# Gate and up of both feed-forward layers as seven block products over two token halves, with the activations kept in DRAM and the down projection as a phase of its own

## The chip, the cores and the metric

The kernel runs on one core of one Trainium2 chip. The time is the device time of one execution in microseconds (us); the times given are the median of several runs. The profile is one further execution, recorded by the hardware profiler.

Engines in the profile: PE is TensorE, whose matmuls do most of the arithmetic, and PEld its weight load; DVE is VectorE, ACT ScalarE, POOL GpSimd, and SP SyncE, which issues the transfers. SBUF is the on-chip memory of the engines, PSUM the accumulators that TensorE writes.

## The reference

Two layers, each a token mixer followed by a SwiGLU feed-forward part, with a norm before and after each. Layer 0 mixes with a gated linear recurrence (RG-LRU), layer 1 with a state-space scan (SSD). There are 1024 prompt tokens and 8 x 16 sample tokens, T = 1152 in all, D = 1024 features and a feed-forward width of 2816 = 22 x 128.

```python
def swiglu(h, w_gate, w_up, w_down):
    return (jax.nn.silu(h @ w_gate) * (h @ w_up)) @ w_down

    ...
        x = x + rmsnorm(mix, p['norm_mix_post'][layer])
        hn = rmsnorm(x, p['norm_ffn_pre'][layer])
        f = swiglu(hn, p['ffn_w_gate'][layer], p['ffn_w_up'][layer], p['ffn_w_down'][layer])
        x = x + rmsnorm(f, p['norm_ffn_post'][layer])
```

Everything is float32, and the products are computed close to float32 accuracy.

## The kernel before

Activations lie with features on the 128 partitions and tokens along the columns. Every float32 operand of a product is split in two parts of TensorE's faster type fp32r: a rounded high part (names ending in h) and the rest (ending in l). A product then takes three matmuls, high by high, high by low and low by high (`mm3`). A weight unit is 128 x 1024: it is loaded raw (`wr`), ScalarE casts its high part (`wh`), and VectorE subtracts for the low part (`wl`). `plan` lists the units in their order of use, and `ahead` and `prepare` keep two raw ones and up to four split ones in flight.

Tokens are worked in three blocks of 384 (`TB`). `gemm` runs 8 feature blocks x 3 matmuls into one of four PSUM buffers named `mm`. In `ffn` (line 783), `up_tb` (line 790) computes for one of the 22 feature tiles and one block the gate and the up product (24 matmuls each), scales the gate by the norm factor `rstd`, applies silu, multiplies by the up product and the factor, and splits the result into `ah` and `al`, which stay in SBUF. `down_tb` (line 804) multiplies a pair of feature tiles by the down weights. The output rows `acc` gather eleven such pairs: the first is copied in by ScalarE, the others are added by VectorE. Down products stand between the up products of the next pairs; the last two pairs are merged, block by block, with `boundary` (line 542).

`boundary` ends a part of a layer for one token block: it normalises the new rows (`mix` or `acc`), adds them to the residual `x`, stores `x`, scales it by the next norm's gain and splits it into `hl`, feature block by feature block. The next layer part's products read `hl`. The factor of the next norm is worked out meanwhile (`npre`, `rs`) and applied to the products.

No instruction is issued where it stands in the program. A recorder takes every operation with the ranges that it reads and writes, computes a latest start for each from an estimate of its cost, counted back from TensorE's sequence, and hands this as a priority to a scheduler, which simulates the engines and fixes the order on each. All instructions thus have the profile's line L330. Each engine then works through its list in order and waits where an operand isn't ready. A tile's buffer comes from a pool with a set number of buffers, and a new tile waits until the last reader of the old one is done: 17 rows of 1180 float32 columns (`rp`), three pairs for `hl` (`ap`).

## Time and profile before

| | before |
| --- | --- |
| median of three runs | 3095.74 us (3092.99 to 3096.46) |
| the profiled execution | 3090.76 us, span 3088.6 us |
| mean granted TensorE clock | 0.981 |
| TensorE busy | 3002.2 us, 17659 matmuls |
| VectorE, ScalarE, GpSimd busy | 1776.4, 965.5, 76.8 us |
| moved by DMA | 263.21 MB, 85 GB/s over the span |
| first and second feed-forward layer | 859.60 and 858.10 us |

A row of the groups gives engine, operation, written tile, read tiles, shape, type and count, then the busy time in us and the mean of one in ns, then the engine's idle time ahead of these instructions and what ended it. A row of the timeline gives start and duration in us; a bracket holds the wait just before it. A row of the stretches gives each engine's busy time in us with its count, the granted clock, and the share and rate of the DMA engines.

### The profile page before, as it was taken

How to read it: one execution, taken by the hardware profiler on the slowest of the kernel's cores; microseconds unless marked ns; L12 is line 12 of the kernel's file. 1: busy time of each engine (PE TensorE's matmuls, PEld its weight loads, DVE VectorE, ACT ScalarE, POOL GpSimd, SP SyncE). 2: the span in 40 equal slices, each digit the busy share in tenths (PEclk: the TensorE clock that was granted, in tenths of full speed). 3: DMA queues.
4: the chain of work that ended last, by engine and by line, in shares of the span. 5: the costliest groups of instructions: out<-in, count | busy, mean ns of one | idle time of the engine just before them, and what ended most of it. 6: DMA issues, size and time to landing. Idle time of an engine off the chain costs nothing.

```text
span 3088.6 us, 42956 instructions
## 1 busy us (share of the span) xinstructions
PE 3002.2 (97%) x17659; PEld 2920.6 (95%) x17659; DVE 1776.4 (58%) x3432; ACT 965.5 (31%) x1441; POOL 76.8 (2%) x176
## 2 busy tenths in 40 slices
PE   8999999999999999999989999999999999999997
PEld 8999999999999999889877988899999999999997
DVE  7765472444444445869978887733663444444436
ACT  5783343111111113445433444322332111111121
POOL 0300000000000000000000000000000000000000
PEclk9999999999999999899999999999999999999998
DMA  3111231111111111335554655432211111111113
GB/s 130 43 35 42 95 111 41 41 42 42 42 41 46 44 44 70 135 116 172 168 169 133 199 174 182 181 134 81 91 67 41 42 41 48 43 42 41 42 35 123
DMA packets 176036, 263.21 MB, mean 85 GB/s; under 512 B 19136, under 2 KB 130112, under 8 KB 175840
## 3 DMA queue, kind: packets, MB, share of 16 engines
q1 hardware_dynamic: 175840, 260.47, 25.0%
q8 instruction: 139, 2.28, 0.3%
q14 instruction: 57, 0.47, 0.0%
HBM read 198.46 MB, written 61.97 MB: 84 GB/s over the span
## 4 chain that ended last, share of the span: by engine, by line
PE 88%; DVE 7%; DMA 2%; ACT 1%; issue 1%; SPq 0%; DVEq 0%; ACTq 0%
PE mm L330 82%; PE aux L330 5%; DVE core L330 1%; DVE acc L330 1%; DVE x L330 1%; DVE hl L330 1%; DMA core<-acd 1%; DVE xc L330 1%; PE one L330 1%; DMA ysc<-core 1%; DMA core<-xbc 1%; DVE wl L330 1%; DVE npre L330 1%; DVE sb L330 0%; DVE silu L330 0%
## 5 line engine op out<-in xcount | busy, mean ns | idle before, releaser
L330 PE MATMUL mm<-hl,wh 128*128 128x384 f32 x7728 | 1991.5, 338 | 30.4 <-DVE hl L330 13.2
L330 PEld LDWEIGHTS mm<-hl,wh 128*128 128x128 f32 x7728 | 1406.2, 190 | 43.2 <-DVE hl L330 18.5
L330 PE MATMUL mm<-hl,wl 128*128 128x384 f32 x3864 | 1294.9, 337 | 0.0
L330 PEld LDWEIGHTS mm<-hl,wl 128*128 128x128 f32 x3864 | 731.5, 189 | 2.7 <-issue 2.7
L330 ACT CAST wh<-wr 128x1024 fp32r<-128x1024 f32 (+1 forms) x218 | 228.2, 1047 | 739.6 <-PE mm L330 737.6
L330 DVE TENSOR_TENSOR acc<-acc,mm 128x384 f32<-128x384 f32 x456 | 248.8, 552 | 199.2 <-PE mm L330 197.5
L330 DVE TENSOR_TENSOR wl<-wr,wh 128x1024 fp32r<-128x1024 f32 (+1 forms) x218 | 265.3, 1217 | 167.4 <-ACT wh L330 167.2
L330 PE MATMUL mm<-ah,wh 128*128 128x384 f32 x1056 | 352.8, 339 | 0.0
L330 PE MATMUL mm<-al,wh 128*128 128x384 f32 x1056 | 350.8, 337 | 0.0
L330 PE MATMUL mm<-ah,wl 128*128 128x384 f32 x1056 | 350.2, 336 | 0.0
L330 DVE TENSOR_TENSOR silu<-silu,mm 128x384 f32<-128x384 f32 x132 | 73.0, 553 | 381.6 <-PE mm L330 380.4
L330 PEld LDWEIGHTS mm<-al,wh 128*128 128x128 f32 x1056 | 198.0, 188 | 0.0
L330 PEld LDWEIGHTS mm<-ah,wh 128*128 128x128 f32 x1056 | 197.9, 188 | 0.0
L330 PEld LDWEIGHTS mm<-ah,wl 128*128 128x128 f32 x1056 | 197.7, 188 | 0.0
L330 DVE TENSOR_TENSOR silu<-mm,rstd 128x384 f32<-128x384 f32 x132 | 73.5, 557 | 211.1 <-PE mm L330 211.1
L330 ACT CAST ah<-silu 128x384 fp32r<-128x384 f32 x132 | 67.8, 514 | 357.3 <-DVE silu L330 357.3
L330 ACT ACTIVATE silu<-silu 128x384 f32<-128x384 f32 x132 | 69.1, 523 | 265.2 <-DVE silu L330 265.2
L330 DVE SCALAR_TENSOR_TENSOR xc<-pad,pvt,xc 128x1176 f32<-128x1176 f32 x96 | 137.1, 1434 | 18.5 <-ACT xc L330 17.9
L330 PE MATMUL aux<-core,core 128*64 128x128 f32 (+1 forms) x1088 | 106.2, 310 | 10.4 <-DVE core L330 6.6
L330 ACT ACT_TABLE_LOAD x74 | 94.9, 1283 | 67.0 <-DVE xc L330 28.9
L330 DVE TENSOR_TENSOR al<-silu,ah 128x384 fp32r<-128x384 f32 x132 | 73.3, 555 | 46.4 <-ACT ah L330 46.4
L330 PEld LDWEIGHTS aux<-core,core 128*64 128x64 f32 (+1 forms) x1088 | 67.5, 145 | 29.2 <-issue 17.2
(142 smaller groups left out, 2351.4 us busy)
## 6 DMA issues: line engine op xcount, KB each, us to landing
wr<-in_wu SPq DMA_DIRECT2D x216, 512.0 KB, 3.5
core<-acd SPq DMA_DIRECT2D x36, 512.0 KB, 5.0
xbc<-pad SPq DMA_DIRECT2D x24, 576.0 KB, 3.3
core<-xbc SPq DMA_DIRECT2D x36, 384.0 KB, 3.7
xs<-x SPq DMA_DIRECT2D x18, 576.0 KB, 3.0
x<-xs SPq DMA_DIRECT2D x18, 576.0 KB, 6.4
ysc<-core SPq DMA_DIRECT2D x36, 256.0 KB, 4.0
y<-ysc SPq DMA_DIRECT2D x16, 576.0 KB, 5.9
```

The source lines that it names most:

```text
L330: op.ins = getattr(getattr(self.nc, op.engine), op.name)(*op.args, **op.kw).ins
```

## The change

Tokens are cut in four quarters of 288 (`QB`), two to each half of 576 (`TH`). The boundaries ahead of the two feed-forward layers still work on blocks of 384, but write their split result into quarters (`Across`, `Quarters`), in two pieces per feature block.

Feature tiles 0 to 3 are computed as before, on quarters, in the order: tiles 0 and 1 on quarters 0 and 1, tiles 2 and 3 on all four, tiles 0 and 1 on quarters 2 and 3, for which their weights are loaded again. For tiles 4 to 21, gate and up together form the product of a 2 x 2 arrangement of weight blocks (gate or up, by half of the features) with a 2 x 2 arrangement of activation blocks (half of the features, by half of the tokens). `strassen` computes it in the form of Strassen and Winograd with seven block products of 12 matmuls instead of eight, once for each quarter of a half (j = 0, 1). It needs sums of activation blocks (`sums`: `x` is loaded back from DRAM, scaled by the gain, added and split; eight times per layer) and sums of weight blocks (`pump`: on GpSimd, in place in the raw tiles, then split into seven items). It combines the products with additions on VectorE and GpSimd (`ep`). Weights are now handled in halves of 512 columns everywhere.

The activations go to DRAM (`act`), in stores of 288 columns, not into `ah` and `al`. After the last tile the down projection runs as a second phase in six chunks, one of two feature tiles and five of four: `load` brings the activations back, ScalarE casts them, VectorE subtracts. The first chunk is copied into `acc` by ScalarE, and the last is merged with `boundary`.

The pools change with it (32 rows; eight half units of `wh` and `wl`, four raw); some parameters of the SSD part are loaded later into the place of others, and the sample states' decay (`bds`) moves into spare columns of other rows.

```diff
+QB = 288
+TH = T // 2
...
-NGF = NFF // 2
+NF0 = 4
+CHUNKS = [[0]] + [[2 * c + 1, 2 * c + 2] for c in range(5)]
...
+        r = [(n, l, f) for f in (0, 1, 2, 3, 0, 1, *range(4, NFF)) for n in ("fg", "fu")]
+        return r + [("fd", l, b, h) for bs in CHUNKS for h in range(2) for b in bs]
...
+        self.cuts = []
+        a, end = tb * TB, (tb + 1) * TB
+        while a < end:
+            b = a // QB
+            e = min(end, (b + 1) * QB)
+            self.cuts.append((Quarters(tiles, b), slice(a - tb * TB, e - tb * TB), slice(a - b * QB, e - b * QB)))
+            for half in range(2):
+                for lo in range(2):
+                    if (b, half, lo) not in tiles:
+                        tiles[b, half, lo] = t.row(F32R, "hq")
+            a = e
...
-        self.wp = ctx.enter_context(tc.tile_pool(name="wp", bufs=4))
-        self.ap = ctx.enter_context(tc.tile_pool(name="ap", bufs=3))
-        self.rp = ctx.enter_context(tc.tile_pool(name="rp", bufs=17))
+        self.wp = ctx.enter_context(tc.tile_pool(name="wp", bufs=8))
+        self.rp = ctx.enter_context(tc.tile_pool(name="rp", bufs=32))
...
+    def half(self, tag, dt):
+        return self.get(self.wp, tag, 512, dt, tag, 4 if tag == "wr" else 8)
...
+    def split_w(self, r):
+        nc = self.nc
+        h, l = self.half("wh", F32R), self.half("wl", F32R)
+        nc.scalar.copy(h, r)
+        nc.vector.tensor_tensor(out=l, in0=r, in1=h.bitcast(F32), op=SUB)
+        return h, l
+    def pump(self):
+        if self.n_entry == len(self.entries):
+            return
+        self.fill()
+        G = self.nc.gpsimd
+        e = self.n_entry
+        u, n = self.entries[e]
+        r, j = self.raws[e], self.n_item
+        done = self.preps.setdefault(u, [])
+        if n == 1:
+            done.append(self.split_w(r[j]))
+        else:
+            b11, b21, b12, b22 = r
+            src = (b11, b12, b12, b21, b11, b21, b22)[j]
+            sub = lambda out, x, y: G.tensor_tensor(out=out, in0=x, in1=y, op=SUB)
+            if j == 1:
+                sub(b11, b12, b11)
+                sub(b12, b22, b12)
+            elif j == 2:
+                sub(b12, b22, b11)
+            elif j == 5:
+                sub(b21, b21, b12)
+            done.append(self.split_w(src))
+        self.n_item += 1
+        if self.n_item == (2 if n == 1 else 7):
+            self.n_item = 0
+            self.n_entry += 1
+            self.raws.pop(e)
+            self.raw_out -= 2 * n
+            self.fill()
...
+    def sums(self, l, j, k, xin, gpre):
+        nc = self.nc
+        V = nc.vector
+        t = self.row(s="sx")[:, :4 * QB]
+        v = t.rearrange("p (i h t) -> p i h t", i=2, h=2)
+        for i in range(2):
+            t0 = i * TH + j * QB
+            nc.sync.dma_start(v[:, i], xin[:, k::4, t0:t0 + QB])
+        for h in range(2):
+            nc.scalar.activation(v[:, :, h], v[:, :, h], AF.Copy, scale=self.pv("g", gpre * 8 + k + 4 * h))
+        a11, a12, a21, a22 = (t[:, n * QB:(n + 1) * QB] for n in range(4))
+        V.tensor_tensor(out=a22, in0=a21, in1=a22, op=ADD)
+        V.tensor_tensor(out=a21, in0=a11, in1=a21, op=SUB)
+        V.tensor_tensor(out=a11, in0=a22, in1=a11, op=SUB)
+        V.tensor_tensor(out=a12, in0=a12, in1=a11, op=SUB)
+        h, lo = self.row(F32R, "sh")[:, :4 * QB], self.row(F32R, "sl")[:, :4 * QB]
+        nc.scalar.copy(h, t)
+        nc.vector.tensor_tensor(out=lo, in0=t, in1=h.bitcast(F32), op=SUB)
+        return {n: tuple(a[:, i * QB:(i + 1) * QB] for a in (h, lo)) for i, n in enumerate(("s2", "s4", "s3", "s1"))}
+    def ffn(self, l, quarters, xin, xout, gin, gpre):
+        nc = self.nc
+        V, A, G = nc.vector, nc.scalar, nc.gpsimd
         self.rs = self.rs_next
...
+        blocks = [Quarters(quarters, b) for b in range(4)]
+        def store(f, t0, a):
+            nc.sync.dma_start(self.act[l][:, f, t0:t0 + QB], a)
+        def up_tb(wg, wu, f, b):
+            pg, pu = self.gemm(wg, blocks[b]), self.gemm(wu, blocks[b])
+            t = self.tmp(QB, s="silu")
+            self.times_rs(t, pg[:, :QB], b * QB, QB)
             A.activation(t, t, AF.Silu)
...
+            V.tensor_tensor(out=t, in0=t, in1=pu[:, :QB], op=MUL)
+            self.times_rs(t, t, b * QB, QB)
+            store(f, b * QB, t)
+        def strassen(w, f, j, step):
+            e = self.row(s="ep")
+            e0, e1, e2, e3 = (e[:, n * QB:(n + 1) * QB] for n in range(4))
+            t1, t2 = j * QB, TH + j * QB
+            X, W = self.psm()[:, :QB], self.psm()[:, :QB]
+            def prod(i, ps, of, first=True):
+                step()
+                wh, wl = w[i]
+                for k in range(4):
+                    c = slice(k * P, (k + 1) * P)
+                    rh, rl = of(k)
+                    mm = nc.tensor.matmul
+                    mm(ps, wh[:, c], rh, start=first and k == 0, stop=False, skip_group_check=True)
+                    mm(ps, wh[:, c], rl, start=False, stop=False, skip_group_check=True)
+                    mm(ps, wl[:, c], rh, start=False, stop=k == 3, skip_group_check=True)
+            plain = lambda b, h: lambda k: tuple(blocks[b].part(4 * h + k, q) for q in range(2))
+            sm = lambda n: lambda k: S[j, k][n]
+            prod(0, X, plain(j, 0))
+            A.copy(e0, X)
+            prod(1, W, sm("s3"))
+            A.copy(e1, W)
+            Y = self.psx()[:, :QB]
+            prod(2, Y, sm("s2"))
+            V.tensor_tensor(out=e0, in0=e0, in1=Y, op=ADD)
+            prod(3, X, plain(j, 1), False)
+            self.times_rs(e3, X, t1, QB)
+            A.activation(e3, e3, AF.Silu)
+            prod(4, W, sm("s1"), False)
+            V.tensor_tensor(out=e2, in0=e0, in1=W, op=ADD)
+            G.tensor_tensor(out=e0, in0=e0, in1=e1, op=ADD)
+            G.tensor_tensor(out=e1, in0=e2, in1=e1, op=SUB)
+            N = self.psx()[:, :QB]
+            prod(5, N, plain(2 + j, 1))
+            V.tensor_tensor(out=e0, in0=e0, in1=N, op=ADD)
+            self.times_rs(e0, e0, t2, QB)
+            A.activation(e0, e0, AF.Silu)
+            V.tensor_tensor(out=e0, in0=e0, in1=e2, op=MUL)
+            self.times_rs(e0, e0, t2, QB)
+            store(f, t2, e0)
+            Q = self.psm()[:, :QB]
+            prod(6, Q, sm("s4"))
+            V.tensor_tensor(out=e1, in0=e1, in1=Q, op=ADD)
+            V.tensor_tensor(out=e1, in0=e1, in1=e3, op=MUL)
+            self.times_rs(e1, e1, t1, QB)
+            store(f, t1, e1)
+        for tb in range(NTB):
+            self.norms[id(blocks[tb])] = self.pres[tb]
+        S = {}
+        for fs, bs in (((0, 1), (0, 1)), ((2, 3), range(4)), ((0, 1), (2, 3))):
+            ws = [(self.take("fg", l, f), self.take("fu", l, f, ahead=f != fs[-1])) for f in fs]
+            for b in bs:
+                for w, f in zip(ws, fs):
+                    up_tb(*w, f, b)
+                    if b == 3 and f == 0:
+                        for _ in range(4):
+                            self.pump()
+            if 2 in fs:
+                for k in range(4):
+                    S[0, k] = self.sums(l, 0, k, xin, gin)
+        for k in range(4):
+            S[1, k] = self.sums(l, 1, k, xin, gin)
+        for f in range(NF0, NFF):
+            w = self.take("fg", l, f)
+            for j in range(2):
+                strassen(w, f, j, self.pump if j else lambda: None)
+        res = []
+        def load(bs):
+            r = []
+            for f in (2 * b + q for b in bs for q in range(2)):
+                a, h, lo = self.row(s="act"), self.row(F32R, "ah"), self.row(F32R, "al")
+                nc.sync.dma_start(a[:, :T], self.act[l][:, f, :])
+                A.copy(h[:, :T], a[:, :T])
+                V.tensor_tensor(out=lo[:, :T], in0=a[:, :T], in1=h[:, :T].bitcast(F32), op=SUB)
+                r.append((h, lo))
+            return r
+        def down_tb(ws, act, h, tb, first):
             c = slice(tb * TB, (tb + 1) * TB)
             for m in range(4):
                 ps = self.psm()
...
+                n = len(act)
+                for q in range(n):
+                    wh, wl = ws[q // 2][q % 2]
+                    cs = slice(m * P, (m + 1) * P)
+                    self.mm3(ps[:, :TB], wh[:, cs], wl[:, cs], act[q][0][:, c], act[q][1][:, c], q == 0, q == n - 1)
                 d = 4 * h + m
...
+                if first:
                     A.copy(acc[d][:, c], ps[:, :TB])
                 else:
                     V.tensor_tensor(out=acc[d][:, c], in0=acc[d][:, c], in1=ps[:, :TB], op=ADD)
...
+        act = load(CHUNKS[0])
+        acc = [self.row(s="acc") for _ in range(KD)]
+        for n, bs in enumerate(CHUNKS):
+            if n < len(CHUNKS) - 1:
+                nxt = load(CHUNKS[n + 1])
+                for h in range(2):
+                    wd = [self.take("fd", l, b, h) for b in bs]
+                    for tb in range(NTB):
+                        down_tb(wd, act, h, tb, n == 0)
+                act = nxt
                 continue
...
+            wd = [[self.take("fd", l, b, h) for b in bs] for h in range(2)]
             for tb in range(NTB):
...
                 for h in range(2):
...
+                    down_tb(wd[h], act, h, tb, False)
+                res.append(self.boundary(tb, acc, xin, l * 4 + 3, gpre, xout))
         return res
```

The order changes most clearly at three places. The first is VectorE's list at the entry of the first feed-forward layer, where the second token block's boundary (`mix`, `x`) splits its result. Before, with `hl` as the split, and `silu` and `al` of the first feature tiles between:

```order
L330 TENSOR_TENSOR x_514<-x_514,mix_451 128x384
L330 SCALAR_TENSOR_TENSOR hl_528<-x_514,pvt,hl_528 128x384
L330 SCALAR_TENSOR_TENSOR mix_452<-mix_452,pvt,aux_516 128x384
L330 TENSOR_TENSOR al_552<-silu_563,ah_551 128x384
L330 TENSOR_TENSOR npre_529<-npre_529,npre_533 128x384
L330 TENSOR_TENSOR silu_566<-silu_566,mm_565 128x384
L330 TENSOR_TENSOR x_515<-x_515,mix_452 128x384
L330 SCALAR_TENSOR_TENSOR hl_528<-x_514,pvt,hl_528 128x384
L330 SCALAR_TENSOR_TENSOR mix_453<-mix_453,pvt,aux_516 128x384
```

And now, with quarters `hq`:

```order
L330 TENSOR_TENSOR x_612<-x_612,mix_571 128x384
L330 SCALAR_TENSOR_TENSOR hq_630<-x_612,pvt,hq_629 128x192
L330 SCALAR_TENSOR_TENSOR mix_572<-mix_572,pvt,aux_614 128x384
L330 SCALAR_TENSOR_TENSOR hq_598<-x_612,pvt,hq_597 128x192
L330 SCALAR_TENSOR_TENSOR rs_655<-rs_655 128x3
L330 TENSOR_TENSOR wl_703<-wr_682,wh_702 128x512
L330 TENSOR_TENSOR npre_631<-npre_631,npre_635 128x384
L330 TENSOR_TENSOR x_613<-x_613,mix_572 128x384
L330 SCALAR_TENSOR_TENSOR hq_630<-x_612,pvt,hq_629 128x192
L330 SCALAR_TENSOR_TENSOR mix_573<-mix_573,pvt,aux_614 128x384
```

Each feature block's split is now two rows of 192 columns for two quarters, and a weight split `wl` stands between the pieces.

The second is VectorE in the middle of a feed-forward layer: before, an up product's steps behind the acc adds,

```order
L330 TENSOR_TENSOR acc_619<-acc_619,mm_883 128x384
L330 TENSOR_TENSOR wl_903<-wr_887,wh_902 128x1024
L330 TENSOR_TENSOR silu_894<-mm_892,rstd_497 128x384
L330 TENSOR_TENSOR silu_894<-silu_894,mm_893 128x384
L330 TENSOR_TENSOR silu_894<-silu_894,rstd_497 128x384
L330 TENSOR_TENSOR al_891<-silu_894,ah_890 128x384
L330 TENSOR_TENSOR silu_897<-mm_895,rstd_497 128x384
```

and now the second quarter of one block-product tile, whose sums (`ep`, from PSUM tiles `mm` and `aux`) alternate with the weight splits of the next tile:

```order
L330 TENSOR_TENSOR wl_990<-wr_976,wh_989 128x512
L330 TENSOR_TENSOR ep_984<-ep_984,aux_991 128x288
L330 TENSOR_TENSOR wl_993<-wr_976,wh_992 128x512
L330 TENSOR_TENSOR wl_995<-wr_975,wh_994 128x512
L330 TENSOR_TENSOR ep_984<-mm_985,rstd_624 128x288
L330 TENSOR_TENSOR wl_997<-wr_974,wh_996 128x512
L330 TENSOR_TENSOR ep_984<-ep_984,mm_986 128x288
L330 TENSOR_TENSOR wl_1000<-wr_975,wh_999 128x512
L330 TENSOR_TENSOR ep_984<-ep_984,aux_998 128x288
```

The acc adds are gone from here, and a weight split comes with nearly every product.

The third is ScalarE at the first down products, which `COPY acc` takes out of PSUM. Before:

```order
L330 CAST wh_629<-wr_609 128x1024
L330 COPY acc_594<-mm_593 128x384
L330 CAST ah_579<-silu_589 128x384
L330 COPY acc_596<-mm_595 128x384
L330 COPY acc_598<-mm_597 128x384
L330 COPY acc_600<-mm_599 128x384
```

And now:

```order
L330 ACTIVATE ep_1344<-ep_1344 128x288
L330 CAST ah_1385<-act_1384 128x1152
L330 CAST ah_1388<-act_1387 128x1152
L330 CAST ah_1391<-act_1390 128x1152
L330 CAST ah_1394<-act_1393 128x1152
L330 COPY acc_1376<-mm_1396 128x384
L330 COPY acc_1377<-mm_1397 128x384
L330 COPY acc_1378<-mm_1398 128x384
```

Four casts of reloaded activations now stand directly ahead of the first copy. On GpSimd, 288 additions and subtractions are new, in a list that had 180 rows.

More of the change, by code (lines that the diff above doesn't have):

```diff
@@ L113 @@
 NPV = _o
+LRU0, SSD0, DT0 = PV["lcw"][0], PV["scw"][0], PV["dtb"][0]
+NPK = LRU0 + max(SSD0 - LRU0, DT0 - SSD0)
 CS = {}
@@ L339, in inside, with __init__, part, pieces @@
     return all(y0 <= x0 and x1 <= y1 for (x0, x1), (y0, y1) in zip(c, b))
+class Block:
+    n = TB
+    def __init__(self, t, s="hl"):
+        self.t = [t.row(F32R, s) for _ in range(5)] + [t.get(t.tp, "last", TB, F32R, s, 3)]
+    def part(self, k, lo):
+        i = k + 8 * lo
+        return self.t[i // 3][:, i % 3 * TB:(i % 3 + 1) * TB]
+    def pieces(self, k):
+        return [(slice(0, TB), self.part(k, 0), self.part(k, 1))]
+class Quarters:
+    n = QB
+    def __init__(self, tiles, b):
+        self.tiles, self.b = tiles, b
+    def part(self, k, lo):
+        return self.tiles[self.b, k // 4, lo][:, k % 4 * QB:(k % 4 + 1) * QB]
+class Across:
+    def __init__(self, t, tiles, tb):
+        self.cuts = []
[9 more added lines that the diff above has]
+            a = e
+    def pieces(self, k):
+        return [(src, q.part(k, 0)[:, dst], q.part(k, 1)[:, dst]) for q, src, dst in self.cuts]
 class Trunk:
@@ new lines, in fill @@
+    def fill(self):
+        while self.n_raw < len(self.entries):
+            u, n = self.entries[self.n_raw]
+            if self.raw_out + 2 * n > 4:
+                return
+            t = []
+            for a in range(n):
+                for h in range(2):
+                    r = self.half("wr", F32)
+                    self.nc.sync.dma_start(r, self.i["wu"][u + a][:, h * 512:(h + 1) * 512])
+                    t.append(r)
+            self.raws[self.n_raw] = t
+            self.raw_out += 2 * n
+            self.n_raw += 1
```

250 lines of the change are left out of this document (105 added, 145 removed).

## The prediction

> **What bounds the kernel now.** I read the page's busy shares and chain first, then the busy time by stretch, then the groups that keep shapes apart.
>
> ```profile
> span 3088.6 us, 42956 instructions
> PE 3002.2 (97%) x17659; PEld 2920.6 (95%) x17659; DVE 1776.4 (58%) x3432; ACT 965.5 (31%) x1441; POOL 76.8 (2%) x176
> PE 88%; DVE 7%; DMA 2%; ACT 1%; issue 1%; SPq 0%; DVEq 0%; ACTq 0%
> ```
>
> TensorE carries 88% of the chain, and its idle time is 3088.6 - 3002.2 = 86.4 us. A change must shorten TensorE's stream or this idle time. The stretches below are the first feed-forward layer (386.20 to 1245.80), 100 us inside it, the SSD mixer, and the second feed-forward layer.
>
> ```profile
> core 0: us, PE busy (x) PEld busy (x) DVE busy (x) ACT busy (x) POOL busy (x), PEclk, DMA share, GB/s
> 386.20:1245.80 859.60, 851.39 (x4881) 847.76 (x4879) 407.25 (x737) 190.81 (x305) 0.00 (x0) 0.99 0.16 54
> 600.00:700.00 100.00, 100.00 (x577) 100.00 (x576) 42.04 (x69) 17.44 (x26) 0.00 (x0) 1.00 0.12 43
> 1334.00:1990.00 656.00, 623.52 (x4040) 555.15 (x4041) 544.74 (x1196) 269.89 (x343) 28.89 (x90) 0.96 0.52 170
> 2217.90:3076.00 858.10, 843.76 (x4842) 841.01 (x4842) 401.24 (x741) 173.83 (x278) 0.00 (x0) 0.99 0.15 52
> ```
>
> Inside a feed-forward layer TensorE never rests and VectorE is under half busy: 577 matmuls of 384 columns in 100 us, so **173.3 ns each**, at a granted clock of 1.00. The two layers, 859.60 + 858.10 us, are the part that the change rewrites. In the SSD mixer VectorE is 544.74/656.00 = 83% busy, so there its work is near the path.
>
> **What the change takes from TensorE.** Both layers together had 2 x 22 feature tiles x 3 token blocks x 2 gemms x 24 = 6336 gate and up matmuls of 384 columns. Now each layer has 4 plain tiles x 4 quarters x 48 = 768 and 18 tiles x 2 x 7 x 12 = 3024 matmuls of 288 columns, 7584 in all. The down projection keeps its 1584 of 384 per layer. In columns, 2433024 become 2184192, 10.2% fewer, but no row has 288. What a matmul of 288 costs decides the case, and rows of other widths bound it:
>
> ```profile
> 1791.28 1.12 PE L330 MATMUL aux<-core,bm 128*128 128x512 f32 x2
> 1797.28 6.17 PE L330 MATMUL aux<-core,bm 128*128 128x512 f32 x14
> 390.93 1.70 PE L330 MATMUL aux<-cs,npost 128*128 128x1 f32 x14
> 393.24 0.51 PE L330 MATMUL aux<-cs,npost 128*128 128x1 f32 x4
> ```
>
> Here fourteen and two plain f32 matmuls of 512 columns differ by (6.17 - 1.12)/12 = 421 ns each, 0.822 ns per column. Ten of one column cost (1.70 - 0.51)/10 = 119 ns each, a floor per instruction. Lower ends: proportional to columns, 173.3 x 288/384 = 130.0 ns; and, if f32 is taken as two passes and the split fp32r type as one (an assumption), half the slope with nothing fixed, 288 x 0.411 = 118.4 ns. Upper end: a straight line from the floor to 384, 119 + (173.3 - 119) x 287/383 = 159.7 ns. My value is half the f32 slope plus what it leaves of 384 columns as a fixed part: 173.3 - 384 x 0.411 = 15.5 ns, 118.4 + 15.5 = **133.9 ns**. I take it because it lies beside the proportional 130.0, and the nearest row (384) is only 96 columns away, the floor 287.
>
> Gate and up: 6336 x 173.3 = 1098.0 us, and 7584 x 133.9 = 1015.5 us: **-82.5 us**. The ends: 130.0 gives -112, 118.4 gives -200, 159.7 gives +113. Break-even without other costs lies at 1098.0/7584 = 144.8 ns.
>
> The Trainium skill (TensorE: Matmul & The Clock Gate, section Back-to-back issue gap) gives N/2.4 + 2.5 ns for a warm matmul; that makes 162.5 ns at 384, where this trace has 173.3, so the trace doesn't agree. For 288 the rule gives 122.5 ns, and the sum would be about 2963 us by it.
>
> **What is added off TensorE.** Costs per operation are from rows of the nearest shape:
>
> ```profile
> L330 DVE TENSOR_TENSOR dt<-aux,pvt 128x288 f32<-128x288 f32 x1 | 0.5, 450 | 0.0
> L330 DVE TENSOR_TENSOR dtq<-aux,dtq 128x288 f32<-128x288 f32 x1 | 0.5, 458 | 3.0 <-ACT dtq L330 3.0
> L330 DVE TENSOR_TENSOR core<-core,dtq 128x512 f32<-128x512 f32 x64 | 43.1, 681 | 0.1
> L330 DVE TENSOR_TENSOR wl<-wr,wh 128x1024 fp32r<-128x1024 f32 x216 | 263.9, 1222 | 164.6 <-ACT wh L330 164.5
> L330 DVE TENSOR_TENSOR xcl<-xc,xch 128x1176 fp32r<-128x1176 f32 x8 | 10.7, 1372 | 0.0
> L330 ACT COPY core<-aux 128x512 f32<-128x512 f32 x4 | 2.3, 581 | 8.4 <-PE aux L330 8.4
> L330 ACT COPY dtq<-aux 128x288 f32<-128x288 f32 x1 | 0.4, 378 | 0.0
> L330 ACT ACTIVATE dtq<-dtq 128x288 f32<-128x288 f32 x1 | 0.4, 444 | 0.0
> L330 ACT CAST xch<-xc 128x1176 fp32r<-128x1176 f32 x8 | 9.1, 1166 | 0.0
> L330 POOL MEMSET core<- 128x256 f32 x4 | 1.6, 404 | 224.7 <-DVE core L330 224.7
> L330 POOL MEMSET pad<- 128x3 f32 x32 | 3.1, 97 | 0.0
> ```
>
> One block-product feature tile lasts 168 x 133.9 = 22.5 us on TensorE. VectorE does 20 operations of 288 at 454 and 7 weight splits of 512 at 681 in it, 13.9 us; ScalarE 7 casts at 581, 4 copies at 378 and 4 silu at 444, 7.4 us. Both are hidden by the products. If the cover were gone, VectorE's share alone would be 36 x 13.9 = 500 us. The eight activation sums per layer (4 x 454 + 1372 = 3.2 us of VectorE each, 25.5 us) lie under the plain stage of 768 x 133.9 = 102.8 us.
>
> GpSimd gets 4 operations of 512 and 4 of 288 per tile; none of its rows has two inputs. Lower end, one stream: (404 - 97)/253 = 1.21 ns per column, so 714 and 443 ns, 4.6 us per tile. Upper end, three streams one after the other: 97 + 3 x 1.21 x columns, 1955 and 1142 ns, 12.4 us. Both fit into 22.5 us, and no product waits for a weight sum made in the same pass: a tile's weights are summed during the second half of the tile before. I take nothing for it. If GpSimd and VectorE exclude each other, see the second rival.
>
> The 512-wide weight halves outside the feed-forward layers cost VectorE 2 x 681 - 1222 = 140 ns more per unit. The mixer's 41 units are 5.7 us on an engine that is 83% busy there: **+5**, with 0 and 10 as ends. The acc adds fall from 216 to 120 per layer, but that work was under the products: nothing.
>
> **The handovers.** First, the entry. Before, three blocks of 384 tokens follow each other as the boundary steps deliver them:
>
> ```profile
> 386.18 0.51 PE L330 MATMUL mm<-hl,wh 128*128 128x384 f32 x2
> 393.44 0.61 DVE L330 SCALAR_TENSOR_TENSOR mix<-mix,pvt,aux 128x384 f32<-128x384 f32 x1
> 407.92 0.51 PE L330 MATMUL mm<-hl,wh 128*128 128x384 f32 x2
> 412.30 0.61 DVE L330 SCALAR_TENSOR_TENSOR hl<-x,pvt,hl 128x384 fp32r<-128x384 f32 x1
> 433.25 0.44 PE L330 MATMUL mm<-hl,wh 128*128 128x384 f32 x1 [1.67 <-DVE hl L330]
> 434.72 0.69 PE L330 MATMUL mm<-hl,wh 128*128 128x384 f32 x1 [0.68 <-DVE hl L330]
> L330 DVE SCALAR_TENSOR_TENSOR hl<-x,pvt,hl 128x384 fp32r<-128x384 f32 x96 | 57.4, 609 | 2.3 <-ACT hl L330 2.2
> ```
>
> The first block runs from 386.18 to 408, and the second's last split comes at 412.9, just in time; block three waits 1.67 + 0.68 = 2.35 us. Now the first quarter has the same 96 matmuls, but 96 x (173.3 - 133.9) = 3.8 us shorter: it ends near 404.3. The second quarter (tokens 288 to 575) needs that same second boundary, whose last split, after its eighth feature block, stays at 412.9; its first gemm could end at 404.3 + 3.2 = 407.5 and ends at 413.3, 5.8 us late. The split now comes in two pieces per feature block (about 0.2 us each of eight, from 609 against 2 x 0.4) and a weight split (681) is queued between them on VectorE, +2.3. Quarter three comes 190 matmuls later, so the old 2.35 us goes (in the second layer 4.3 by the same reading). Net 8.1 - 2.4 and 8.1 - 4.3: **+10** for both; ends 0 and 24.
>
> Second, the first block products wait for activation sums loaded back from DRAM: **+3** for both layers, ends 0 and 8. Third, the down phase. ScalarE has four casts of 1152 columns queued ahead of the copy that frees the first of four PSUM buffers. They belong to the second chunk and wait for its loads:
>
> ```profile
> wr<-in_wu SPq DMA_DIRECT2D x216, 512.0 KB, 3.5
> x<-xs SPq DMA_DIRECT2D x18, 576.0 KB, 6.4
> yr<-ysd SPq DMA_DIRECT2D x16, 576.0 KB, 9.4
> L330 ACT COPY acc<-mm 128x384 f32<-128x384 f32 x72 | 34.2, 478 | 73.0 <-PE mm L330 73.0
> ```
>
> The four PSUM buffers cover 4 x 6 x 173.3 = 4.2 us of the first chunk's products. The loads' rows come free with the last tiles' epilogue (some 4.5 us after the last product, an estimate: ten operations of 454), the loads land 6.4 us later, and the last cast needs 1.2: 12.1 - 4.2 = 7.9, with the copy 478 ns more, 8.5 per layer: **+17**; ends 0 (rows free early) and 2 x (4.5 + 9.4 + 4 x 1.17 - 4.2) = 29. Behind these casts stand only the acc copies, for which TensorE waits.
>
> Sum: -82.5 + 10 + 3 + 17 + 5 = -47.5. The profiled execution took 3090.76 us (span 3088.6), so 3043.3; the median of the three runs lies 4.98 above it: **3048 us**.
>
> **Rivals.** (1) The handovers eat the gain. Each at its upper end: 24 + 8 + 29 + 10 = 71, and 11 more if the same quarter waits recur after the reload of tiles 0 and 1: 82, time 3095. For it: every handover goes through VectorE or ScalarE queues in fixed order. Against: they would all have to be at their ends. (2) Slower: GpSimd and VectorE exclude each other on SBUF, so that a tile costs their sum. At the upper end 13.9 + 12.4 = 26.3 > 22.5 us, 3.8 us a tile, 36 tiles, +137: 3185. It decides from 8.6 us of GpSimd per tile on, and the gain is gone at 9.9. For it: in the feed-forward layers before GpSimd did nothing (0.00 busy), so no row shows them together there. Against: in the mixer both run at VectorE's 83% with unremarkable durations. (3) The pace lies on the line from the floor, 159.7: 3090.8 + 113 + 35 + 5 = 3244. Against: weight loads are identical and 384 columns show no floor. (4) The fixed part is hidden, 118.4 ns: 3090.8 - 200 + 35 + 5 = 2931, and values between 118 and 130 lead to 2931 to 3019.
>
> For rival 2 the Trainium skill (SBUF — State Buffer, section Who interferes with whom) says that a VectorE instruction with two SBUF inputs contends with a GpSimd instruction that reads SBUF, while transfers don't. Of VectorE's 27 operations in a tile, 17 have two SBUF inputs; no run here shows the effect.
>
> **How the numbers follow.** Chances: forecast 0.77, rival (1) 0.07, (2) 0.08, (3) 0.03, (4) 0.05. The forecast's own range is 3019 (130.0 ns) to 3080 (two handovers at their ends). The range 2985 to 3092 adds part of (4) and most of (1). A measurement of this kernel can tell 0.2%, 6.2 us, from no change: faster means under 3089.5. The forecast, (4) and a quarter of (1) give 0.84 faster; most of the rest of (1), 0.04 the same; (2), (3) and what is left of (1) 0.12 slower.
>
> **What would show it.** Right: 288-column matmuls at 134 ns in a window inside the block products, with VectorE near 62% and ScalarE near 33% there; one stall near 405 of 6 to 8 us behind a split, one of 8 us where the down products start, behind an ACT copy. Wrong: TensorE idle in the middle of the block products, with VectorE operations of 288 far over 460 ns beside GpSimd ones (rival 2), or a pace off 134 by more than 4 ns, which moves the time by 7.6 us for each ns.

## The result, and the profile after

The changed kernel takes **3043.22 us** (median of four runs, 3037.95 to 3046.33) where the kernel before takes 3094.36 beside it: a ratio of 0.9836 with a 95% interval of 0.9815 to 0.9857. The forecast was 3048, in a range of 2985 to 3092. The profiled execution has a span of 3044.6 us, 44.0 less than before. First the page's head for the changed kernel:

```profile
span 3044.6 us, 48917 instructions
PE 2920.6 (96%) x18907; PEld 2844.1 (93%) x18907; DVE 2038.7 (67%) x4041; ACT 1166.6 (38%) x1983; POOL 406.1 (13%) x464
```

TensorE is busy 81.6 us less (3002.2 before) and idle 37.6 us more (124.0, where it was 86.4). The next two views are busy time by stretch. The first is of the changed kernel: the first feed-forward layer, the SSD part, the second feed-forward layer, 100 us inside the block products, and the stretch from near the end of the first layer's plain stage to the end of its block products. The granted clock (PEclk) is the share of its full clock that TensorE was given.

```profile
core 0: us, PE busy (x) PEld busy (x) DVE busy (x) ACT busy (x) POOL busy (x), PEclk, DMA share, GB/s
391.46:1207.85 816.39, 799.85 (x5462) 797.95 (x5462) 521.80 (x967) 274.54 (x514) 164.26 (x144) 0.98 0.29 94
1207.85:2197.71 989.86, 943.09 (x5870) 875.11 (x5870) 734.37 (x1648) 398.02 (x614) 38.44 (x108) 0.97 0.44 146
2197.71:3019.61 821.90, 802.48 (x5463) 799.81 (x5463) 524.44 (x978) 266.22 (x498) 162.17 (x144) 0.98 0.28 94
600.00:700.00 100.00, 100.00 (x757) 100.00 (x756) 72.75 (x122) 33.59 (x68) 41.38 (x37) 1.00 0.24 80
500.00:915.00 415.00, 415.00 (x3132) 415.00 (x3131) 297.02 (x509) 146.69 (x288) 163.68 (x144) 1.00 0.24 80
```

And the two feed-forward layers of the kernel before, cut at the same instructions (first product of the layer, last down product):

```profile
386.18:1231.59 845.41, 842.77 (x4838) 841.07 (x4838) 393.51 (x710) 182.78 (x291) 0.00 (x0) 0.99 0.14 50
2217.90:3061.49 843.59, 839.12 (x4815) 837.02 (x4815) 389.39 (x709) 172.79 (x276) 0.00 (x0) 0.99 0.14 47
```

The layers are 29.0 and 21.7 us shorter. TensorE's busy time in them falls by 79.6 us, its waits rise from 7.1 to 36.0. The part ahead of the first layer is 5.3 longer (391.46 against 386.18), the SSD part 3.6 (989.86 against 986.31), the end 2.1 shorter. Inside the block products TensorE never waits: 757 matmuls of 288 columns in 100 us are **132.1 ns** each. What it waits for, over the whole execution (sum, times, longest):

```profile
PE mm L330 <- ACT acc L330: 20.9, 2, 10.5
PE mm L330 <- DVE hq L330: 14.3, 9, 3.4
...
PE mm L330 <- ACT hl L330: 8.5, 1, 8.5
PE mm L330 <- DVE dtr L330: 6.7, 1, 6.7
```

The first row is the start of the two down phases, the second the entry of the two layers, the third the start of the program, the fourth lies at the start of the SSD part.

### The profile page after: what moved, and what is told of

It is laid out like the page before. It is cut to its first block, busy times and chain, and to the rows that moved or that the text cites. A ratio compares the mean times of both kernels' runs of the same rounds, so it can differ in the third digit from the quotient of the medians.

```text
span 3044.6 us, 48917 instructions
## 1 busy us (share of the span) xinstructions
PE 2920.6 (96%) x18907; PEld 2844.1 (93%) x18907; DVE 2038.7 (67%) x4041; ACT 1166.6 (38%) x1983; POOL 406.1 (13%) x464
## 4 chain that ended last, share of the span: by engine, by line
PE 47%; DMA 3%; DVE 3%; issue 0%; ACT 0%; SPq 0%; DVEq 0%; POOL 0%; ACTq 0%
PE mm L330 38%; PE aux L330 8%; DMA ysc<-core 1%; DVE core L330 1%; DMA core<-acd 1%; DMA core<-xbc 1%; PE one L330 0%; DVE xc L330 0%; DVE acc L330 0%; DVE x L330 0%; DMA act<-act 0%; DVE wl L330 0%; DVE hq L330 0%; DVE sb L330 0%; SPq L330 0%
## 5 line engine op out<-in xcount | busy, mean ns | idle before, releaser
L330 PE MATMUL mm<-hl,wh 128*128 128x384 f32 x3504 | 914.2, 342 | 22.3 <-ACT hl L330 8.5
L330 PEld LDWEIGHTS mm<-hl,wh 128*128 128x128 f32 x3504 | 639.3, 189 | 30.2 <-ACT hl L330 15.4
L330 ACT CAST wh<-wr 128x512 fp32r<-128x512 f32 (+1 forms) x559 | 335.4, 618 | 678.4 <-PE mm L330 613.9
L330 PE MATMUL mm<-hl,wl 128*128 128x384 f32 x1752 | 589.0, 340 | 0.0
L330 DVE TENSOR_TENSOR wl<-wr,wh 128x512 fp32r<-128x512 f32 (+1 forms) x559 | 422.4, 768 | 142.0 <-ACT wh L330 114.9
L330 PE MATMUL mm<-hq,wh 128*128 128x288 f32 x2176 | 450.3, 300 | 14.4 <-DVE hq L330 14.3
L330 PE MATMUL mm<-ah,wh 128*128 128x384 f32 x1056 | 353.9, 340 | 20.9 <-ACT acc L330 20.9
L330 PEld LDWEIGHTS mm<-hq,wh 128*128 128x128 f32 x2176 | 356.3, 191 | 17.2 <-DVE hq L330 16.7
L330 PEld LDWEIGHTS mm<-hl,wl 128*128 128x128 f32 x1752 | 330.7, 189 | 2.0 <-issue 2.0
L330 PE MATMUL mm<-hq,wl 128*128 128x288 f32 x1088 | 325.0, 299 | 0.0
L330 PE MATMUL mm<-sl,wh 128*128 128x288 f32 x864 | 255.1, 295 | 0.0
L330 PEld LDWEIGHTS mm<-sh,wl 128*128 128x128 f32 x864 | 162.5, 188 | 0.0
```

Source lines behind the costliest of these rows:

```text
L330: op.ins = getattr(getattr(self.nc, op.engine), op.name)(*op.args, **op.kw).ins
```

## The experiments

My theory was: the time is the number of matmuls times their pace, plus waits at the handovers; work on VectorE, ScalarE and GpSimd is hidden as long as the products run. The rivals were a gain that comes from elsewhere, and contention of GpSimd and VectorE. Edits are to the changed kernel unless the text says otherwise.

### Are the seven products the gain? All tiles plain

```diff
-NF0 = 4
+NF0 = 22
...
-        for f in range(NF0, NFF):
-            w = self.take("fg", l, f)
-            for j in range(2):
-                strassen(w, f, j, self.pump if j else lambda: None)
+        for f in range(4, NFF):
+            w = self.take("fg", l, f), self.take("fu", l, f)
+            for b in range(4):
+                up_tb(*w, f, b)
```

> The changed kernel with all 22 feature tiles computed plainly on quarters of 288: no block products and no sums, everything else (activations in DRAM, second phase) kept. Theory: the gain is the number of matmuls times their pace. Gate and up rise from 3792 to 4224 matmuls per layer, 2 x 432 x 132.3 ns = +114 us: about 3157 us, slower than the kernel before. Rival: the gain comes from the narrower blocks or from the separate down phase, and the block products are worth little: 3043 us within 10. Both: the two waits of 10.5 us at the down phase stay.

Measured: 3141.43 us, ratio to before 1.0148 (1.013 to 1.0166): slower than the kernel before. A stretch inside the first layer of this kernel:

```profile
600.00:900.00 300.00, 300.00 (x2267) 300.00 (x2266) 96.78 (x190) 50.27 (x95) 0.00 (x0) 1.00 0.21 66
```

2267 matmuls in 300 us are again 132.3 ns each. So the narrower blocks alone lose: 8448 matmuls of 132.3 are 1117.7 us against 1098.0 before. The products' count is the gain. It came out 16 us below the expected number, and the trace says why: the two waits behind `ACT acc` (20.9 us) are gone here, against what I had written for both sides. With no block products there are no `sh`, `sl` and `ep` rows at the end of the layer that the loads could wait for; that this is the reason is argued, not tried, and the loads-first kernel below speaks against it: there the rows are free in time.

### What does TensorE wait for at the down phase?

In the changed kernel, ScalarE and then TensorE at the first down phase:

```profile
918.44 1.16 ACT L330 CAST ah<-act 128x1152 fp32r<-128x1152 f32 x1 [0.80 <-DMA act<-act]
924.63 1.15 ACT L330 CAST ah<-act 128x1152 fp32r<-128x1152 f32 x1 [5.03 <-DMA act<-act]
927.13 1.15 ACT L330 CAST ah<-act 128x1152 fp32r<-128x1152 f32 x1 [1.35 <-DMA act<-act]
928.51 1.15 ACT L330 CAST ah<-act 128x1152 fp32r<-128x1152 f32 x1 [0.23 <-DMA act<-act]
929.57 1.62 ACT L330 COPY acc<-mm 128x384 f32<-128x384 f32 x4
...
919.38 0.34 PE L330 MATMUL mm<-ah,wl 128*128 128x384 f32 x1
930.09 0.69 PE L330 MATMUL mm<-ah,wh 128*128 128x384 f32 x1 [10.38 <-ACT acc L330]
```

This is what the order showed: four casts stand ahead of the copies, each waits for its load, and TensorE stands still when four PSUM buffers are full. I first moved the casts behind the copies:

```diff
-                A.copy(h[:, :T], a[:, :T])
+                o = A.copy(h[:, :T], a[:, :T])
+                if len(bs) > 1 and bs[0] == 1:
+                    o.after.append(copies[-1])
...
-                nxt = load(CHUNKS[n + 1])
+                nxt = load(CHUNKS[n + 1]) if n else None
...
                         down_tb(wd, act, h, tb, n == 0)
+                    if nxt is None:
+                        nxt = load(CHUNKS[1])
```

> The changed kernel, with the casts of the second chunk's activations ordered behind the first twelve copies into acc. Theory: ScalarE's queue order is what TensorE waits for, so both waits of 10.4 and 10.5 us at the down phase go: about 21 us, 3022 us (ratio to the changed kernel 0.993). Rival: the wait only moves, to the second chunk, whose operands then come late (a wait behind ah or al some 25 us later): 3035 to 3043 us.

Measured: 3046.69 us, ratio 0.9844 (0.9829 to 0.9859), no better than the change itself. The wait only moved, as the rival said, but not to where it said: it is not behind `ah` or `al` of the second chunk, but still behind `acc`, and the time lies above the rival's range. ScalarE's casts and TensorE in this kernel, two thirds through the first chunk:

```profile
927.67 1.16 ACT L330 CAST ah<-act 128x1152 fp32r<-128x1152 f32 x1
933.43 1.15 ACT L330 CAST ah<-act 128x1152 fp32r<-128x1152 f32 x1 [4.61 <-DMA act<-act]
...
938.72 0.69 PE L330 MATMUL mm<-ah,wh 128*128 128x384 f32 x1 [7.64 <-ACT acc L330]
```

The wait is still there, and still between the first cast and the second lie 5.8 us (6.2 before the edit). That looks like a chain: the second load comes only at about the time when the first tile is cast. The cause is in the recorder: buffers of one pool are given out in order of first use, and each row's first writer is ordered behind that of the row before. `load` asked for the rows in the order act, ah, al, act, ah, al, so the scheduler placed the second load behind the first subtraction. The chain acts through this fixed order, not through a wait for a cast at run time: from 890 to 945 in the changed kernel the queue of transfers waits 27.6 us behind `wl`, 13.9 behind `ep` and 5.4 behind `wr`, and never behind `ah` or `al`. The loads stand in the queue behind weight loads and stores that wait for these. The next kernel asks for all four `act` rows first.

```diff
-            r = []
+            r, raw = [], []
             for f in (2 * b + q for b in bs for q in range(2)):
-                a, h, lo = self.row(s="act"), self.row(F32R, "ah"), self.row(F32R, "al")
-                nc.sync.dma_start(a[:, :T], self.act[l][:, f, :])
+                raw.append(self.row(s="act"))
+                nc.sync.dma_start(raw[-1][:, :T], self.act[l][:, f, :])
+            for a in raw:
+                h, lo = self.row(F32R, "ah"), self.row(F32R, "al")
```

> The changed kernel with the four loads of a chunk recorded ahead of its casts, so that their buffers are given out first. In the changed kernel every next load waits until the rows of the one before have been cast and subtracted, because buffers are given out in order of first use. Theory: this chain makes the casts late (the last landed 13 us after the block products ended), and they stand ahead of the acc copies; with the loads first the wait of 10.4 and 10.5 us falls to 0 to 3 each: 3043 - 17 = 3026 us. Rival: the rows themselves come free only with the last products, so the loads start as late as now: 3040 us or more.

Measured: **3028.22 us**, ratio 0.9786 (0.9767 to 0.9805), against 3026 expected. The queue's loads of the second chunk in the changed kernel, one by one:

```profile
914.48 0.38 SPq L330 DMA_DIRECT2D act<-act  x1
...
919.60 0.42 SPq L330 DMA_DIRECT2D act<-act  x1
...
921.92 0.87 SPq L330 DMA_DIRECT2D act<-act  x2
```

And the queue and ScalarE in this kernel:

```profile
908.20 2.11 SPq L330 DMA_DIRECT2D act<-act  x4
...
917.78 1.16 ACT L330 CAST ah<-act 128x1152 fp32r<-128x1152 f32 x1
918.85 0.61 ACT L330 CAST wh<-wr 128x512 fp32r<-128x512 f32 x1
919.36 1.61 ACT L330 COPY acc<-mm 128x384 f32<-128x384 f32 x4
```

All four loads are issued at 908.20, before the products end; the copies start at 919.36, where they started at 929.57. The casts still stand ahead of the copies, and TensorE's two waits behind `acc` fall from 20.9 us to 3.0 in all. So the place in ScalarE's list, on which the prediction rested, was only where the lateness showed; the loads were late because they were chained by the order of their buffers.

### Do VectorE and GpSimd hold each other up?

```diff
-        G = self.nc.gpsimd
+        G = self.nc.vector
...
-        V, A, G = nc.vector, nc.scalar, nc.gpsimd
+        V, A, G = nc.vector, nc.scalar, nc.vector
```

> The changed kernel with all weight sums and product sums moved from GpSimd to VectorE. Theory: beside GpSimd, VectorE's operations with two SBUF inputs are longer (ep by rstd 651 ns, against 453 for silu by rstd of the same shape), but off the path: without GpSimd they return to about 455 and 681 ns, VectorE does 13.9 + 4.5 = 18.4 us in a tile of 22.3, and the time stays at 3043 within 6 us. Rival 1, the two engines' contention costs TensorE time: faster by 10 us or more. Rival 2, VectorE at 82% is too full and TensorE waits for sums or weights: slower by 10 us or more, with waits behind wl or ep.

Measured: 3049.53 us, ratio 0.9854 (0.984 to 0.9869): the same as the change within what these runs tell apart (the intervals of the two ratios overlap; 6.3 us is just outside the theory's 6). VectorE, which now does GpSimd's work as well, is busy 75.6 us of 100 inside the block products, where it was 72.8. The groups that tell the story, of the changed kernel:

```profile
L330 POOL TENSOR_TENSOR wr<-wr,wr 128x512 f32<-128x512 f32 x144 | 197.6, 1372 | 978.3 <-DVE wl L330 427.2 <-DMA sx<-xs 407.2 <-issue 79.6
L330 DVE TENSOR_TENSOR ep<-ep,rstd 128x288 f32<-128x288 f32 x216 | 135.1, 651 | 1.2
L330 POOL TENSOR_TENSOR ep<-ep 128x288 f32<-128x288 f32 x144 | 129.0, 896 | 187.3 <-DVE ep L330 158.3 <-ACT wh L330 19.7 <-ACT ep L330 3.6
L330 DVE TENSOR_TENSOR ep<-ep 128x288 f32<-128x288 f32 x144 | 80.4, 599 | 0.1
L330 DVE TENSOR_TENSOR ep<-ep,aux 128x288 f32<-128x288 f32 x144 | 64.7, 449 | 115.4 <-PE aux L330 103.5 <-issue 7.2 <-POOL ep L330 3.3
```

and of this kernel, where GpSimd has none of it:

```profile
L330 DVE TENSOR_TENSOR ep<-ep,aux 128x288 f32<-128x288 f32 x144 | 64.8, 450 | 25.8 <-issue 19.1 <-DMA act<-ep 3.2 <-PE aux L330 0.7
L330 DVE TENSOR_TENSOR ep<-ep,rstd 128x288 f32<-128x288 f32 x216 | 92.1, 451 | 1.2
L330 DVE TENSOR_TENSOR ep<-ep 128x288 f32<-128x288 f32 x288 | 125.2, 453 | 6.2 <-ACT ep L330 0.2
```

With both inputs in SBUF an operation takes 651 or 599 ns beside GpSimd and 451 or 453 without it; with one input in PSUM (`aux`) it takes 449 and 450. So the two engines do hold each other up, and of these operations only those with two SBUF inputs are longer. The rule of the Trainium skill (SBUF — State Buffer, section Who interferes with whom), which the prediction weighed, agrees with these rows in kind. In the `ep` rows it costs VectorE (216 x 0.200 + 144 x 0.146)/36 = 1.8 us of a tile's 22.2, off the path.

How far it is from the path, the next kernel asked. It makes two of the weight differences three times.

```diff
-                sub(b11, b12, b11)
-                sub(b12, b22, b12)
+                for _ in range(3):
+                    sub(b11, b12, b11)
+                for _ in range(3):
+                    sub(b12, b22, b12)
```

> The changed kernel with the first two weight differences of each tile done three times (the result is the same up to rounding), 4 more GpSimd operations of 512 per tile: GpSimd rises from 9.1 to about 14.6 us of a tile's 22.3. The weight sums have some 9 us of slack before they are needed. Theory: VectorE and GpSimd only lengthen each other's operations off the path: 3043 within 6 us. Rival: they exclude each other whenever VectorE has two SBUF inputs (17 operations, 9.3 us per tile); then 14.6 + 9.3 = 23.9 exceeds 22.3, 1.6 us for 36 tiles, +58: 3100 us.

Measured: 3074.80 us, ratio 0.9943 (0.9926 to 0.996): 31.6 us slower than the change, 0.9 per tile. Both sides missed. The same group, and TensorE's new wait, in this kernel:

```profile
L330 DVE TENSOR_TENSOR ep<-ep,aux 128x288 f32<-128x288 f32 x144 | 64.7, 449 | 126.1 <-POOL ep L330 121.0 <-PE aux L330 3.7 <-PE mm L330 1.4
...
PE mm L330 <- ACT ep L330: 9.5, 16, 1.5
```

VectorE now waits 121.0 us in all for GpSimd's `ep`, where it was 3.3. GpSimd works its list in order, and the product sums, which a product's end needs, stand behind the added differences:

```profile
643.28 5.57 POOL L330 TENSOR_TENSOR wr<-wr,wr 128x512 f32<-128x512 f32 x4 [3.34 <-DVE ep L330]
648.80 0.80 POOL L330 TENSOR_TENSOR ep<-ep 128x288 f32<-128x288 f32 x1
```

I had counted the slack of the weight sums and overlooked what is queued behind them. The weight sums come late as well: TensorE also waits 8.0 us in all behind `wh` and `wl`, which are none of its waits in the changed kernel. GpSimd at 9.1 us of a tile is free, at the 14.7 measured here it is not. VectorE's own operations grow, too: `ep` by `rstd` takes 843 ns, where it was 651. How much of the 0.9 us is the shared access and how much the queue stays open.

### The entry of a layer

```diff
+        cuts = [slice(0, TB // 2), slice(TB // 2, TB)] if quarters is not None and tb == 1 else [slice(0, TB)]
+        for i, s in enumerate(cuts):
+            pieces = lambda k: hl.pieces(k) if len(cuts) == 1 else hl.pieces(k)[i:i + 1]
...
+                order.append(V.tensor_tensor(out=x[:, s], in0=x[:, s], in1=r[:, s], op=ADD))
```

> The changed kernel, with the boundary of the second token block done in two passes of 192 columns, the pass for the second quarter first. Theory: TensorE's 14.3 us of waits behind hq at the two entries come from VectorE doing all 384 columns of a feature block before the next; the first pass is ready some 6 us earlier, for 16 more operations of about 0.2 us. The waits fall to 2 to 6 us: 3043 - 10 = 3033 us. Rival: the second pass and the third block's boundary come 3 us later and are waited for instead: 3040 to 3046 us.

Measured: 3054.86 us, ratio 0.9878 (0.9863 to 0.9893), slower than the change by 11.6. The waits behind `hq` fall from 14.3 us to 1.9, as the theory said, and one larger wait has taken their place in each layer (11.3 us in the second):

```profile
426.82 1.41 PE L330 MATMUL one<-cs,npre 128*128 128x1 f32 x6 [14.92 <-DVE npre L330]
```

That is the sum for the next norm's factor. It needs all 384 columns of the block, which now come last, and it stands early in TensorE's list. I read part of the entry's price as VectorE's work itself, not its order: the quarter needs its factor as well as its splits.

### A shorter plain stage, and the start

Both kernels here have the loads-first edit. The first also orders two weight casts at the program's start behind ScalarE's first work on the activations:

```diff
-            nc.scalar.copy(wh[:, c], r[:, c])
+                later.append((wh, wl, r, c))
...
+        hl = nc.ops[hl]
+        for p in later[1:]:
+            cast(*p).after.append(hl)
```

> The changed kernel with the loads of a chunk first, and at the program's start the casts of the first weight's second and third piece ordered behind ScalarE's first work on the activations. In the changed kernel a cast that waits for its load stands ahead of that work, and the first matmul starts at 8.5 us where it was 6.0 before. Theory: both gains add, 3028 - 2.5 = 3025.5 us. Rival: the first matmuls then wait for the weights instead: 3028 us.

Measured: **3024.49 us** (five runs), ratio 0.9777 (0.9764 to 0.979), the fastest of all here. Of the two edits only the loads count: the first matmul still starts at 8.3 us, because ScalarE's list then had two `npost` squares ahead of `hl`, and the second waits for its own load. The start stays unmended. The second kernel has two plain tiles in place of four:

```diff
-NF0 = 4
+NF0 = 2
...
-        for fs, bs in (((0, 1), (0, 1)), ((2, 3), range(4)), ((0, 1), (2, 3))):
+        for fs, bs in (((0, 1), range(4)),):
```

> As the one with the loads first and the start mended, with two plain feature tiles in place of four, each on all four quarters in a row, so that no weights are loaded twice. Theory: two more tiles per layer take 168 matmuls of 132.3 ns in place of 192: 3.2 us x 2 x 2 = 12.7 us less, 3013 us. Rival: the plain stage of 51 us is too short a cover for the sums and the third block's boundary, and TensorE waits for sh or sl or hq: 3020 to 3035 us.

Measured: 3076.74 us, ratio 0.9942 (0.993 to 0.9955), 52 slower than with four plain tiles. The rival was right in kind, and its price was too low. TensorE at the first block products:

```profile
492.35 0.61 PE L330 MATMUL aux<-sh,wh 128*128 128x288 f32 x1 [8.11 <-ACT sh L330]
493.75 0.61 PE L330 MATMUL aux<-sl,wh 128*128 128x288 f32 x1 [0.79 <-DVE sl L330]
497.05 0.61 PE L330 MATMUL aux<-sh,wh 128*128 128x288 f32 x1 [2.46 <-ACT sh L330]
```

Each product waits for the next sum, 32.9 us in all behind `sh` and `sl`; TensorE's granted clock is 0.70 from 480 to 520, which adds to the waits. Four plain tiles are not waste: they are the cover for the eight sums. The sums come late with their transfers: the last loads of activations for the first layer's sums (`sx`) are issued at 480.11, and ScalarE waits 5.7 us for them. Whether another order of the transfers would do with less cover, no run tries.

### Narrower matmuls

Each plain-tile matmul of the changed kernel is done here as two of 144 columns. This changes how the plain tiles accumulate, so their values, and the outputs that depend on them, are not the reference's; only the pace is read.

```diff
+        if ps.shape[-1] == QB:
+            for c in (slice(0, QB // 2), slice(QB // 2, QB)):
+                p = mm(ps[:, c], wh, rh[:, c], start=first, stop=False, skip_group_check=True)
```

> The changed kernel, with each matmul of the plain tiles (768 per layer) done as two of 144 columns. From 384 columns at 173.3 and 288 at 132.3 the line is 0.427 ns per column and 9.3 fixed, so 144 would take 70.8 ns: 1536 x (141.6 - 132.3) = +14 us, 3057 us. Rival: a floor of 119 ns per instruction, as the matmuls of one column showed: 1536 x (238 - 132.3) = +162 us, 3205 us.

Measured, in one run: 3471.41 us, far beyond both. The start of the first layer's plain stage, and a later stretch of it:

```profile
391.31:396.63 5.32, 5.32 (x49) 5.32 (x49) 4.40 (x15) 3.34 (x9) 0.00 (x0) 1.00 0.78 227
450.00:500.00 50.00, 50.00 (x236) 50.00 (x236) 29.28 (x60) 22.94 (x32) 0.00 (x0) 0.50 0.36 113
```

At first, at a granted clock of 1.00, the 48 matmuls of 144 columns take 111 ns each (the 49th of the row is another): far from the line's 70.8, and near the 119 that rows of one column gave. From about 400 on the clock is at 0.50 to the end of the stage, though TensorE never waits in it, and 236 matmuls in 50 us are 212 ns each. With 288 columns the same stage had 1.00 (440 to 500). At 111 ns throughout, the edit would cost 1536 x (222 - 132.3) = +138 us, an estimate; the other 290 of the 428 us are then the halved clock. Why the clock falls, this one run does not show. So columns can't be cut much further: two matmuls of 144 take 1.7 times one of 288 even at full clock.

### Where the operands lie

In the changed kernel the matmuls of 384 columns outside the feed-forward layers are slower, too: 520 in the 90 us from 290 to 380, in the LRU part, where 527 were done before. Two kernels made from the kernel before ask why. The first puts each `hl` into six tiles in place of one:

```diff
-        t = self.get(self.ap, "big", 2 * KD * TB, F32R, s)
-        return t[:, :KD * TB], t[:, KD * TB:]
+        return Rows(self, s)
```

> The kernel before, with its hl and gh in six separate tiles each, as in the changed kernel, in place of one tile that holds both parts. The changed kernel's matmuls of 384 columns in the LRU and SSD stages take 175 ns where those of before take 173.3. Theory: where the moving operand lies sets this, so hl at 175 ns costs 11592 x 1.7 = +20 us: 3114 us. Rival: it comes from the weights' halves or from something else in the changed kernel, and this one stays at 3094 within 5.

Measured: 3094.99 us, ratio 1.0004 (0.9994 to 1.0014). The split by itself does nothing; the tiles here were 4608 bytes, so each still starts at the same place within 512 bytes (9 x 512). The second shifts the low weights and `hl` by 128 bytes:

```diff
         w = [self.get(self.wp, "wh", 1024, F32R, "wh")]
+        pad = self.get(self.wp, "wpad", 32, F32, "wpad", 1)
+        nc.gpsimd.memset(pad, 0.0)
```

> The kernel before with 128 bytes left free between the high and the low weight tiles (and one small buffer less for the conv states). In the kernel before all hl, wh and wl buffers start at one residue of 512 bytes and its matmuls take 173.3 ns; ah and al rows, which lie at four residues, take 175 there, and in the changed kernel all operands lie so. Splitting hl into six tiles at the same residue left 173. Theory: different residues cost 1%: 11592 matmuls at 175, +20 us: 3114 us. Rival: the residue does nothing: 3094 within 5 us.

Measured: 3116.11 us, ratio 1.0073 (1.0055 to 1.0091), as the theory had it. In the middle of the first feed-forward layer, where the kernel before has 577 matmuls:

```profile
600.00:700.00 100.00, 100.00 (x571) 100.00 (x570) 42.17 (x68) 17.50 (x26) 0.00 (x0) 1.00 0.13 43
```

175.1 ns in place of 173.3. In the 90 us from 290 to 380 this kernel does 519 matmuls, like the changed kernel's 520. The changed kernel keeps the activations that TensorE reads mostly in rows of 1180 columns, 4720 bytes, which is no multiple of 512, so they do not all start alike. That this slows its LRU part follows from the likeness; no run moves the operands of the changed kernel. Only one shift, 128 bytes, was tried, so 512 as the period that counts is not shown.

## Why the prediction was right, point by point

- **TensorE's stream.** Forecast 133.9 ns per matmul of 288 and -82.5 us. Measured 132.1 to 132.3, which alone would be 7584 x 132.3 = 1003.4 us, -94.6; TensorE's busy time in the two layers fell by 79.6. The difference of 15 us lies behind the waits: right after the wait at 930.09 the matmuls are 0.32 us apart for nine of them, where 0.175 is usual, at a granted clock of 0.50, and the granted clock over the two entries is 0.82 and 0.77, where it was 0.92 and 0.91. The sum had charged waits by their length alone. Term mis-sized twice, in opposite directions; that they nearly cancel is luck.
- **Entry.** Forecast 8.1 us per layer, of which 2.4 and 4.3 were there before: +10. Measured 14.3 against 6.65, +7.6. The named place and releaser are right.
- **First block products.** Forecast +3, measured 0: the sums are ready, and with two plain tiles the missing cover costs 52 us.
- **Down phase.** Forecast 8.5 per layer behind the casts, measured 10.4 and 10.5. The place and the releaser were right, the reason (rows come free some 4.5 us after the last product) was not: the loads-first kernel issues all four loads at 908.20, before the products end. The loads were chained through the order of their buffers. That the number came near is luck.
- **SSD part.** Forecast +5, measured +3.6. I had put all of it to VectorE's weight halves, and the trace does not show that: VectorE's busy time in this part is 734.4 us, where it was 736.3, and TensorE waits nowhere in it behind `wl`. TensorE's idle time rises by 5.4 us in all, with new waits of 6.7 behind `dtr` (the scan's raw step sizes) and 6.5 behind `rs` and less elsewhere. So the number is near by luck, and its cause stays open; what part the operands' place has, no run separates.
- **What was not forecast.** The part ahead of the first layer is 5.3 us longer, 5.0 of it idle time of TensorE. The first matmul starts 2.5 us later (8.5 against 6.0). Even stretches of the LRU part run 1% slower, by the padded kernel most likely because of where the operands lie.
- **Cover.** Forecast 13.9 us of VectorE and 4.6 to 12.4 of GpSimd per tile of 22.5. Measured 16.2 and 9.2 in 22.2 (72.75 and 41.38 in 100 us). Hidden, as forecast, though VectorE's rows with two SBUF inputs are 0.15 to 0.2 us longer than those I took. One half of the sign for rival 2 thus came true, operations of 288 far over 460 ns; the other, TensorE idle in the block products, did not.
- **Rivals.** Handovers eating the gain: no, though the waits in the two layers grew by 29 us. GpSimd against VectorE: the contention is there, and has no price at this load; its point in the prediction (8.6 us of GpSimd) charged all of VectorE's 27 operations, and only 17 are concerned; GpSimd's 9.2 us are past that point. The pace on a line from the floor, 159.7, and a hidden fixed part, 118.4: both off; the two measured points lie 0.43 ns per column apart, with some 9 ns fixed. By the Trainium skill (TensorE: Matmul & The Clock Gate, section Back-to-back issue gap), whose formula is for a matmul by itself, 288 columns would take 122.5 ns; in this trace's stream, with a weight load for each matmul, they take 132.1, as 384 took 173.3 and not 162.5.
- **Sums.** The upper end of the forecast's own range, two handovers at their ends, adds up to 3074 and not 3080 (24 - 10 + 29 - 17 = 26 above 3048). The time doesn't rest on it.

## What to carry to other kernels

Count what an algebraic saving takes from the bound engine by the measured pace of the narrower shape, and stop narrowing where it no longer falls in step with the columns. Then look at each seam of the new plan for what the next stage needs first: here most of the loss at the down phase came from the order in which buffers were asked for, and one reordered loop, all loads before the first cast, was worth 15 us. Work that looks like waste beside the saving (four plain tiles) may be the cover for its preparation.

## What the runs showed of the hardware that I had not expected

- In a stage of 144-column matmuls TensorE's granted clock fell to 0.50 some 9 us in and stayed there to the stage's end, though TensorE never waited; with 288 columns it had 1.00 in the same place (440 to 500). One run, and the cause is open.
- A matmul of 144 columns took 111 ns at a granted clock of 1.00, one of 288 took 132.1.
- Matmuls of 384 columns took 173.3 ns where all operands start at one place within 512 bytes, and 175.1 after a shift of the low weights and the activations by 128 bytes, in a stream without waits.
- A VectorE operation on 288 columns with two SBUF inputs takes 451 to 453 ns alone and 599 to 651 beside GpSimd's additions and subtractions (644 to 843 where GpSimd does more); with one input in PSUM it takes 449 to 450 either way.
